# Two mixer layers on one core: output gate summed on VectorE and spread by a transfer, with a new work list

## Chip, core and metric

One core of a Trainium2 chip runs the whole program. The metric is device time in microseconds, the median of several runs. Engine names are those of the profile: PE (matmul), PEld (its weight loads), DVE (vector), ACT (scalar), POOL (GpSimd), SP (the engine whose queue issues every transfer here).

## What is computed

Two layers (DEPTH 2) over 512 latent tokens and 256 context tokens, width 1024. In each layer the normalised and modulated input goes through one wide projection, three attention branches run side by side, each branch is multiplied by a SiLU gate path and projected to 1024, the three are merged by sigmoid gates, and an output projection follows. Shift, scale and **gate** of a layer come from one vector product:

```python
shift, scale, gate = jnp.split(jax.nn.silu(c) @ w_ada[l] + b_ada[l], 3, axis=-1)
h = rms_norm(x, norm_g[l]) * (1.0 + scale[:, None]) + shift[:, None]
...
y = (jax.nn.sigmoid(g_na) * ((o_na * jax.nn.silu(z_na)) @ w_br_l[0])
     + jax.nn.sigmoid(g_mla) * ((o_mla * jax.nn.silu(z_mla)) @ w_br_l[1])
     + jax.nn.sigmoid(g_diff) * ((o_diff * jax.nn.silu(z_diff)) @ w_br_l[2]))
x_new = x + gate[:, None] * (y @ w_out_l)
```

The context stream has its own gate (from c_ctx) and is updated in layer 0 alone. All numbers are float32.

## The kernel before, in words

A float32 product of accuracy is made of three PE products of split operands: every operand is a pair (hi, lo), and `mm3` issues lines 115, 116 and 117. Weights are loaded in units of 128x384 (`ws`, line 138), copied to hi by ACT (line 122) and subtracted to lo by DVE or POOL (line 127).

A layer has twelve steps, one for each pair of heads of the kinds D, M, N in turn. A step of `mixer` records, in this order: the attention of the step before (`attn_group`: scores L712 or L754, softmax, transposes L702, products with V L833 or L867), the projection of this step (`proj_nd` or `proj_m`, PSUM banks `pj`; transposes L473, L662), its SiLU path (`zgate`), some strips of the merge gates (`gm`, 24 in a layer, as many a step as the table `NGM` says), and some halves of the next modulation vectors (`ada_half`, at the steps that `ADA` lists: eight products of `sT` with two weight tiles `aw` of 512 KB, line 237, then the four partial sums of a 256-wide chunk go to `rowsd` in DRAM). `zgate`, `gm` and `ada_half` share one PSUM bank, `fl`: the next user waits until DVE (`zs`, L414), ACT (`th`, L1011) or DVE (`arow`, L239) has read the last one's.

After the steps: for `NE[l]` of the eight output strips the branches 2 and 1 are projected (`branch`) while the last attention runs; then branch 0 of these strips and all three branches of the rest; each finished strip is split into `y` (L122, L127); then `out_proj`, which multiplies by `gate` (L1059), adds to x and stores.

The order on each engine is not the order of recording. Every call sets a priority with `at` (the step's base, plus `PRI` for the kind of work, plus `SHIFT` for single steps), and a scheduler that models the engines picks, while the program is built, what each engine does next by priority and readiness. Each engine then runs its list strictly in order; so does SP's queue of transfers. `NGM`, `SHIFT`, `ADA`, `PRI` and `NE` are thus the **work list**.

The gate before: `ada_gate` (L278) runs after the branches. For each half of 512 columns it loads the partial sums, nine rows with the bias (`arow`, one buffer), and PE multiplies them by a 0/1 matrix `selb`, which sums the rows and spreads the sum over 128 partitions at once (L292); ACT scales it into `gate` (L293). Layer 0 has two streams, layer 1 one: six products of 512 columns, which the profile counts as twelve, since each float32 one is recorded as two.

Of the kernel before, what the change touches and what calls it, by code (L numbers as in the profile page):

```python
# [7 lines left out]
F32 = mybir.dt.float32  # L8
F32R = mybir.dt.float32r
AF = mybir.ActivationFunctionType  # L10
ALU = mybir.AluOpType
AX = mybir.AxisListType

BACC = dict(dynamic_dma_scratch_size=1024)
P = 128
D = 1024
# [10 lines left out]
NEG = -1e30  # L27
BAND = (0, 64, 192, 256)
QTYPE = (0, 1, 1, 2)
NGM = ((1, 3, 0, 2, 4, 0, 0, 4, 3, 2, 3, 2), (0, 4, 1, 0, 2, 1, 1, 4, 2, 3, 4, 2))  # L30

SHIFT = {(12, 'gm'): -1000, (8, 'zg'): -300, (18, 'gm'): -1000, (13, 'attn'): 300, (9, 'zg'): -300, (5, 'pm'): -600, (6, 'attn'): -1000, (23, 'zg'): -600, (8, 'attn'): 150, (10, 'gm'): -1000, (8, 'gm'): -1000}
ADA = ((4, 5, 5, 5, 7, 7, 8, 8, 8, 8, 10, 11), (4, 4, 6, 6))

C_ID = 0
C_ONE = 128
# [12 lines left out]
def f(ap):  # L49
    return ap.bitcast(F32)  # L50


class Mixer:
# [26 lines left out]
    def at(self, key, i=0):  # L80
        o = self.PRI[key] + SHIFT.get((self.where, key), 0)
        self.tc.cur_priority = self.base + o + i * self.PRI["step"] // 20

# [14 lines left out]
    ONE, PF, VG, MR = False, '', '', False  # L98
    COPY, NORM = 'D', 'g'
    PH = ""  # L100
    PRI = dict(step=2200, attn=500, prep=1000, pm=1500, pn=1200, zg=1500, gm=2500, ada=2500, us=300, br=2700)
    ORDER = ('DMNDMNDMNDMN', 'DMNDMNDMNDMN')
    GRP = (0, 1, 2)
    PREP = 0
# [173 lines left out]
    def ada_gate(self, l, pool):  # L278
        nc = self.nc
        strs = (0, 1) if l == 0 else (0,)  # L280
        gate = [pool.tile([P, D], F32, tag=f"gate{s}", bufs=1, name=f"gate{l}_{s}") for s in strs]
        selb = pool.tile([9, 2, P], F32, tag="selb", bufs=1, name=f"selb{l}")
        nc.sync.dma_start(selb, self.io["selb"])
        for hf in range(2):
            rows = pool.tile([9, 512], F32, tag="arow", bufs=1, name=self.n("arow"))
            src = self.rowsd[l][4 + hf].rearrange("k (g r) n -> g r k n", g=4)
            for s in range(2):
                nc.sync.dma_start(rows[4 * s:4 * s + 4, :].rearrange("g (k n) -> g k n", k=4), src[:, s])
            nc.sync.dma_start(rows[8:9, :], self.io["b_gate"][l:l + 1, hf * 512:(hf + 1) * 512])
            for s in strs:  # L290
                ps = self.bk()
                nc.tensor.matmul(ps, selb[:, s, :], rows[0:9, :], start=True, stop=True)  # L292
                nc.scalar.mul(gate[s][:, hf * 512:(hf + 1) * 512], ps, 0.25)  # L293
        return gate

    def bias_gather(self, l):
# [577 lines left out]
    POOLS = dict(pt2=1, th=1, qn=2, sq=2, t2=2, c2=2, c3=2, kr=2, krt=2, mss=2, ssr=2, ss=2)  # L874
    BUFS = dict(pf=1, mr=1, arow=1, qk=6, kl=1, V=5, P=3, pt4=4, pt2=2, zs=2, ut=3, sq=1, ss=4, qn=3, st=3, t2=1, r0=2, th=1, c2=2, c3=1, mss=4, krt=2, Vs=1, bias=1, kr=1, ssr=1)
    BI = {"N": 0, "M": 1, "D": 2}
    NE = (3, 8)

    def open(self, name, side="left"):
        c = self.tc.tile_pool(name=name, bufs=1, side=side, reuse_waits="tile")  # L880
# [2 lines left out]
    def mixer(self, l):  # L883
        tc = self.tc
        ud = self.dram.tile([3, 4, P, NTOK], F32, name=f"ud{l}")
        self.th = self.dram.tile([24, P, NTOK], F32, name=f"thd{l}")
        cs, ps = zip(*(self.open(f"p1{x}_{l}") for x in "abc"))
        pool = _Pool(ps, self.BUFS, self.POOLS)
        gms = list(range(24))
        ada = [(0, 4), (0, 5), (1, 2), (1, 0), (1, 3), (1, 1)] if l == 0 else [(1, 4), (1, 5)]  # L890
        ada = [(*c, hf) for c in ada for hf in range(2)]
        self.base = tc.cur_priority
        br = {"D": self.dtab, "N": dict(pool=pool), "M": None}
        self.kl = pool.tile([P, 2, NTOK], F32R, tag="kl", name=f"kl{l}")
        for m in range(2):
            self.nc.gpsimd.memset(f(self.kl[64 - 64 * m:128 - 64 * m, m]), 0.0)
        prev = None
        seen = dict(D=0, M=0, N=0)
        for step, kind in enumerate(self.ORDER[l]):
            pr = seen[kind]  # L900
            self.where = 12 * l + step
            if l == 0 and step in (0, 6):
                self.bias_gather(step // 6)
            if kind == "N" and pr == 0:
                self.flush()
            seen[kind] += 1
            if prev:
                self.at("attn")
                self.attn(l, *prev, pool, ud)
            if step == self.PREP:  # L910
                self.at("prep")
                self.nbg = self.NB[1]
                br["M"] = self.mla_prep(l, pool, pool)
                self.nbg = self.NB[2]
            if kind == "M":
                self.at("pm")
                a = self.proj_m(l, pr, pool, br[kind])
            else:
                self.at("pn")
                a = self.proj_nd(l, kind, pr, pool, br[kind])  # L920
            self.at("zg")
            prev = (kind, pr, a, self.zgate(l, 4 * self.BI[kind] + pr, None, pool))
            for g in range(NGM[l][step]):
                self.at("gm", g)
                self.gm(l, gms.pop(0), pool)
            for i in range(ADA[l].count(step)):
                self.at("ada", 10 * i)
                self.ada_half(*ada.pop(0), pool)
            self.base += self.PRI["step"]
        assert not gms and not ada  # L930
        for c in cs[:0:-1]:
            c.__exit__(None, None, None)
        self.hctx.__exit__(None, None, None)
        cu, pu = self.open(f"p2u_{l}", "right")
        cx, px = self.open(f"p2x_{l}", "right")
        cf, self.pf2 = self.open(f"p2f_{l}", "right")
        self.at("attn")
        self.attn(l, *prev, pool, ud)
        us = {}
        self.at("us")  # L940
        for b in (2, 1):
            us[b] = self.uload(l, ud, b, pu, px)
        yf = []
        for n in range(self.NE[l]):
            self.at("br", n)
            yf.append(self.branch(l, n, (2, 1), us, px, None, (self.pj, self.fl)))
        cs[0].__exit__(None, None, None)
        tc.cur_priority = self.base + 6000
        cy, py = self.open(f"p2_{l}")
        o = self.cols(l)[0][0]  # L950
        y = [py.tile([P, KT, NTOK], F32R, name=f"y{l}_{j}") for j in range(2)]
        cn, pn = self.open(f"p2n_{l}")
        us[0] = self.uload(l, ud, 0, pn, px)
        for n in range(KT):
            if n < self.NE[l]:
                v = self.branch(l, n, (0,), us, px, yf[n], (self.pj, self.fl, self.bk))
            else:
                v = self.branch(l, n, (2, 1, 0), us, px, None, (self.pj, self.fl, self.bk))
            for c0, w in self.cols(l):
                c = slice(c0, c0 + w)  # L960
                self.split(y[0][:, n, c], y[1][:, n, c], v[:, c0 - o:c0 - o + w], "a", "v")
        gate = self.ada_gate(l, py)
        for c in (cn, cf, cx, cu):
            c.__exit__(None, None, None)
        self.out_proj(l, y, gate)
        cy.__exit__(None, None, None)
# [12 lines left out]
    def branch(self, l, n, bs, us, pool, yf, banks):  # L979
# [3 lines left out]
        if first:  # L983
            yf = self.pf2.tile([P, NTOK - o], F32, tag="yf", bufs=self.NE[l], name=self.n("yf"))
        for b in bs:
# [204 lines left out]
```

## Time and profile before

| what | value |
|---|---|
| median of 3 runs | 1928.85 us (1923.16, 1928.85, 1929.49) |
| the profiled execution | 1923.38 us, its span 1921.6 us |
| granted PE clock, mean | 0.993 |
| PE busy | 1857.9 us (97%) |
| PEld busy | 1725.0 us (90%) |
| DVE, ACT, POOL busy | 1192.0, 938.8, 762.1 us |
| transfers | 245.38 MB, all issued by SP |

The span runs from the first to the last instruction; the execution's own time is 1.8 us longer. PE's rows are pipelined: a product's row lasts longer than the distance to the next one, so the cost of a product is read from the distance of two starts.

### The profile page before, as it was taken

Reading aid. Unit: us, or ns where it says so; the run is one execution under the profiler, and the core shown is the slowest. Engines: PE = TensorE matmul, PEld = TensorE weight load, DVE = VectorE, ACT = ScalarE, POOL = GpSimd, SP = SyncE. Lnnn points to the kernel's source line nnn. Section 1 sums busy time; section 2 is a strip of 40 time slices with the busy share of each in tenths; the row PEclk is TensorE's granted clock in tenths of the full one; section 3 lists DMA queues with packets and bytes.
Section 4 is the critical chain, followed back from the end, with each engine's and each line's share of the span. In section 5 each row is a group of like instructions: output and inputs, shape, how many; then the busy total and the mean of one; then the engine's idle time right before and its main releaser. Section 6 shows DMA issues by size and latency. Waiting matters only on the chain.

```text
span 1921.6 us, 33888 instructions
## 1 busy us (share of the span) xinstructions
PE 1857.9 (97%) x11707; PEld 1725.0 (90%) x11707; DVE 1192.0 (62%) x2698; ACT 938.8 (49%) x2422; POOL 762.1 (40%) x1057
## 2 busy tenths in 40 slices
PE   7999999999999999999999999999899999999998
PEld 3999999999899998999999988898799798889878
DVE  4556567646865655557663455668668665766763
ACT  4445455445644544546432344556456455555531
POOL 3343333233433333243355454444334343443363
PEclk8999999999999999999999999999999999999999
DMA  9454223343545334324655234423522523442663
GB/s 314 159 178 142 64 67 100 102 132 86 159 136 169 85 120 134 103 89 120 228 161 171 99 122 132 122 75 91 167 64 71 161 78 92 123 131 60 192 194 117
DMA packets 184824, 245.38 MB, mean 128 GB/s; under 512 B 22454, under 2 KB 148040, under 8 KB 184652
## 3 DMA queue, kind: packets, MB, share of 16 engines
q1 hardware_dynamic: 184652, 243.21, 41.1%
q8 instruction: 93, 1.52, 0.3%
q14 instruction: 79, 0.65, 0.1%
HBM read 190.45 MB, written 46.53 MB: 123 GB/s over the span
## 4 chain that ended last, share of the span: by engine, by line
PE 87%; DVE 4%; DMA 3%; ACT 2%; POOL 2%; issue 1%; SPq 0%; ACTq 0%; DVEq 0%; POOLq 0%
PE pj L115 11%; PE pj L117 11%; PE pj L116 11%; PE fl L115 10%; PE fl L116 10%; PE fl L117 9%; PE sc L712 6%; PE bk L867 4%; PE bk L702 4%; PE bk L833 2%; PE sc L754 1%; PE pj L662 1%; DMA aw<-in_w_ada 1%; PE pj L473 1%; PE fl L237 1%
## 5 line engine op out<-in xcount | busy, mean ns | idle before, releaser
L122 ACT CAST w<-ws 128x384 fp32r<-128x384 f32 (+3 forms) x520 | 237.4, 473 | 256.2 <-PE fl L116 153.0
L127 POOL TENSOR_TENSOR w<-ws,w 128x384 fp32r<-128x384 f32 (+3 forms) x260 | 242.5, 938 | 298.3 <-ACT w L122 275.3
L115 PE MATMUL fl<-h,w 128*128 128x384 f32 (+1 forms) x864 | 314.4, 364 | 6.4 <-DVE zs L414 4.7
L115 PE MATMUL pj<-w,h 128*128 128x384 f32 (+2 forms) x944 | 313.6, 335 | 2.0 <-DVE kl L127 1.1
L117 PE MATMUL fl<-h,w 128*128 128x384 f32 (+1 forms) x864 | 310.7, 360 | 2.2 <-DVE w L127 1.3
L116 PE MATMUL pj<-w,h 128*128 128x384 f32 (+2 forms) x944 | 309.8, 329 | 1.0 <-POOL w L127 1.0
L116 PE MATMUL fl<-h,w 128*128 128x384 f32 (+1 forms) x864 | 310.0, 359 | 0.0
L117 PE MATMUL pj<-w,h 128*128 128x384 f32 (+2 forms) x944 | 309.2, 331 | 0.7 <-POOL h L127 0.6
L127 DVE TENSOR_TENSOR w<-ws,w 128x384 fp32r<-128x384 f32 (+2 forms) x260 | 170.6, 659 | 72.4 <-ACT w L122 67.2
L167 POOL TENSOR_TENSOR ss<-ss,nhalf 128x4 f32<-128x4 f32 (+1 forms) x144 | 143.1, 994 | 177.8 <-DVE ss L166 161.7
L717 ACT ACTIVATE P<-sc,st 128x768 f32<-128x768 f32 (+1 forms) x192 | 159.5, 832 | 100.8 <-DVE st L798 43.0
L764 POOL TENSOR_SCALAR P<-P,st 128x512 f32<-128x512 f32 (+1 forms) x128 | 107.9, 845 | 241.1 <-DVE st L760 211.4
L115 PEld LDWEIGHTS pj<-w,h 128*128 128x128 f32 x944 | 178.5, 190 | 8.9 <-issue 3.0
L117 PEld LDWEIGHTS pj<-w,h 128*128 128x128 f32 x944 | 177.7, 189 | 5.7 <-DVE h L368 3.3
L115 PEld LDWEIGHTS fl<-h,w 128*128 128x128 f32 x864 | 163.1, 189 | 20.2 <-DVE zs L414 6.5
L116 PEld LDWEIGHTS pj<-w,h 128*128 128x128 f32 x944 | 179.1, 190 | 1.7 <-POOL w L127 1.3
L706 DVE TENSOR_TENSOR pt<-bk,pt 128x512 fp32r<-128x512 f32 (+1 forms) x256 | 147.5, 585 | 52.1 <-ACT pt L705 49.6
L117 PEld LDWEIGHTS fl<-h,w 128*128 128x128 f32 x864 | 162.9, 189 | 14.0 <-POOL w L127 1.6
L116 PEld LDWEIGHTS fl<-h,w 128*128 128x128 f32 x864 | 163.1, 189 | 9.5
L705 ACT CAST pt<-bk 128x512 fp32r<-128x512 f32 (+1 forms) x256 | 127.2, 507 | 77.0 <-PE bk L702 73.9
L712 PE MATMUL sc<-qk,qk 96*128 96x512 f32 (+3 forms) x592 | 144.3, 337 | 1.4 <-ACT P L717 1.0
L702 PE MATMUL bk<-cst,P 128*128 128x128 f32 x832 | 128.9, 273 | 5.0 <-DVE ss L166 2.0
(239 smaller groups left out, 3915.5 us busy)
## 6 DMA issues: line engine op xcount, KB each, us to landing
ws<-in_w_qkv SPq DMA_DIRECT2D x128, 192.0 KB
ws<-in_w_gm SPq DMA_DIRECT2D x96, 192.0 KB
aw<-in_w_ada SPq DMA_DIRECT2D x32, 512.0 KB
ct<-cqd SPq DMA_DIRECT2D x40, 384.0 KB
ct<-ckd SPq DMA_DIRECT2D x48, 256.0 KB
ws<-in_w_z SPq DMA_DIRECT2D x48, 192.0 KB
thd<-th SPq DMA_DIRECT2D x48, 192.0 KB
ws<-in_w_br SPq DMA_DIRECT2D x48, 192.0 KB
```

Of the source, the lines that this page charges most:

```text
L115: mm(out, a[0], b[0], start=first, stop=False)
L116: mm(out, a[0], b[1], start=False, stop=False)
L117: mm(out, a[1], b[0], start=False, stop=last)
L122: nc.scalar.copy(hi, src)
L127: (nc.gpsimd if le == "g" else nc.vector).tensor_tensor(lo, src, f(hi), ALU.subtract)
L167: nc.gpsimd.tensor_tensor(out, out, self.nhalf[:, :cols], ALU.pow)
L702: nc.tensor.transpose(pt[:, i * P:(i + 1) * P], src[:, (b0 + i) * P:(b0 + i + 1) * P], self.ident)
L705: nc.scalar.copy(h, v)
L706: nc.vector.tensor_tensor(lo, v, f(h), ALU.subtract)
L712: mm(s[:, d0:d0 + w], x, y, start=i == 0, stop=i == len(ops) - 1)
L717: nc.scalar.activation(p, src, AF.Exp, bias=st[:, m:m + 1], accum_out=st[:, o:o + 1])
L764: nc.gpsimd.tensor_scalar(p, p, st[:, 4 + m:5 + m], 0.0, ALU.mult, ALU.add)
```

## The change

1. `ada_gate` no longer uses PE or ACT. The four partial sums and the bias go to 8 partitions a stream (`grow`), one DVE reduction adds the five, one DVE instruction scales by 0.25, the 8x128 result is stored to DRAM (`gated`), and a transfer per stream reads it back with every partition reading the same 4 KB (`gate`, 128x1024, 512 KB written). `selb` is no longer loaded.
2. `ada_gate` is called ahead of the branch-0 loop instead of behind it.
3. The work list: `NGM`, `SHIFT`, `ADA`, `PRI["br"]` (2700 to 2600) and `NE` ((3, 8) to (3, 6)) have other values. The number of products in all is the same, apart from the gate's.

```diff
@@ -27,10 +27,10 @@
 NEG = -1e30
 BAND = (0, 64, 192, 256)
 QTYPE = (0, 1, 1, 2)
-NGM = ((1, 3, 0, 2, 4, 0, 0, 4, 3, 2, 3, 2), (0, 4, 1, 0, 2, 1, 1, 4, 2, 3, 4, 2))
-
-SHIFT = {(12, 'gm'): -1000, (8, 'zg'): -300, (18, 'gm'): -1000, (13, 'attn'): 300, (9, 'zg'): -300, (5, 'pm'): -600, (6, 'attn'): -1000, (23, 'zg'): -600, (8, 'attn'): 150, (10, 'gm'): -1000, (8, 'gm'): -1000}
-ADA = ((4, 5, 5, 5, 7, 7, 8, 8, 8, 8, 10, 11), (4, 4, 6, 6))
+NGM = ((1, 3, 0, 2, 3, 0, 0, 4, 3, 2, 3, 3), (1, 4, 0, 0, 2, 1, 1, 4, 1, 3, 4, 3))
+
+SHIFT = {(12, 'gm'): -1000, (8, 'zg'): -150, (18, 'gm'): -1000, (13, 'attn'): 300, (9, 'zg'): -300, (5, 'pm'): -600, (6, 'attn'): -1000, (23, 'zg'): -600, (8, 'attn'): 600, (10, 'gm'): -1000, (8, 'gm'): -1000, (20, 'zg'): -300, (15, 'ada'): 300, (9, 'gm'): 600, (11, 'attn'): 600, (3, 'attn'): 1000, (4, 'attn'): -300}
+ADA = ((5, 5, 5, 6, 7, 7, 8, 8, 8, 9, 10, 11), (4, 4, 6, 6))
 
 C_ID = 0
 C_ONE = 128
@@ -98,7 +98,7 @@
     ONE, PF, VG, MR = False, '', '', False
     COPY, NORM = 'D', 'g'
     PH = ""
-    PRI = dict(step=2200, attn=500, prep=1000, pm=1500, pn=1200, zg=1500, gm=2500, ada=2500, us=300, br=2700)
+    PRI = dict(step=2200, attn=500, prep=1000, pm=1500, pn=1200, zg=1500, gm=2500, ada=2500, us=300, br=2600)
     ORDER = ('DMNDMNDMNDMN', 'DMNDMNDMNDMN')
     GRP = (0, 1, 2)
     PREP = 0
@@ -278,19 +278,20 @@
     def ada_gate(self, l, pool):
         nc = self.nc
         strs = (0, 1) if l == 0 else (0,)
+        n = 8 * len(strs)
         gate = [pool.tile([P, D], F32, tag=f"gate{s}", bufs=1, name=f"gate{l}_{s}") for s in strs]
-        selb = pool.tile([9, 2, P], F32, tag="selb", bufs=1, name=f"selb{l}")
-        nc.sync.dma_start(selb, self.io["selb"])
-        for hf in range(2):
-            rows = pool.tile([9, 512], F32, tag="arow", bufs=1, name=self.n("arow"))
-            src = self.rowsd[l][4 + hf].rearrange("k (g r) n -> g r k n", g=4)
-            for s in range(2):
-                nc.sync.dma_start(rows[4 * s:4 * s + 4, :].rearrange("g (k n) -> g k n", k=4), src[:, s])
-            nc.sync.dma_start(rows[8:9, :], self.io["b_gate"][l:l + 1, hf * 512:(hf + 1) * 512])
-            for s in strs:
-                ps = self.bk()
-                nc.tensor.matmul(ps, selb[:, s, :], rows[0:9, :], start=True, stop=True)
-                nc.scalar.mul(gate[s][:, hf * 512:(hf + 1) * 512], ps, 0.25)
+        gd = self.dram.tile([n, P], F32, name=f"gated{l}")
+        raw = pool.tile([n, 5, P], F32, tag="grow", bufs=1, name=self.n("grow"))
+        src = self.rowsd[l][4:6].rearrange("c k (g r) n -> (c k) g r n", g=4)
+        for s in strs:
+            nc.sync.dma_start(raw[8 * s:8 * s + 8, 0:4], src[:, :, s])
+            nc.sync.dma_start(raw[8 * s:8 * s + 8, 4], self.io["b_gate"][l].rearrange("(k n) -> k n", n=P))
+        tot = pool.tile([n, P], F32, tag="gtot", bufs=1, name=self.n("gtot"))
+        nc.vector.tensor_reduce(tot, raw.rearrange("p g n -> p n g"), AX.X, ALU.add)
+        nc.vector.tensor_scalar(tot, tot, 0.25, None, ALU.mult)
+        nc.sync.dma_start(gd, tot)
+        for s in strs:
+            nc.sync.dma_start(gate[s], gd[8 * s:8 * s + 8].rearrange("k n -> (k n)").unsqueeze(0).to_broadcast([P, D]))
         return gate
 
     def bias_gather(self, l):
@@ -874,7 +875,7 @@
     POOLS = dict(pt2=1, th=1, qn=2, sq=2, t2=2, c2=2, c3=2, kr=2, krt=2, mss=2, ssr=2, ss=2)
     BUFS = dict(pf=1, mr=1, arow=1, qk=6, kl=1, V=5, P=3, pt4=4, pt2=2, zs=2, ut=3, sq=1, ss=4, qn=3, st=3, t2=1, r0=2, th=1, c2=2, c3=1, mss=4, krt=2, Vs=1, bias=1, kr=1, ssr=1)
     BI = {"N": 0, "M": 1, "D": 2}
-    NE = (3, 8)
+    NE = (3, 6)
 
     def open(self, name, side="left"):
         c = self.tc.tile_pool(name=name, bufs=1, side=side, reuse_waits="tile")
@@ -951,6 +952,7 @@
         y = [py.tile([P, KT, NTOK], F32R, name=f"y{l}_{j}") for j in range(2)]
         cn, pn = self.open(f"p2n_{l}")
         us[0] = self.uload(l, ud, 0, pn, px)
+        gate = self.ada_gate(l, py)
         for n in range(KT):
             if n < self.NE[l]:
                 v = self.branch(l, n, (0,), us, px, yf[n], (self.pj, self.fl, self.bk))
@@ -959,7 +961,6 @@
             for c0, w in self.cols(l):
                 c = slice(c0, c0 + w)
                 self.split(y[0][:, n, c], y[1][:, n, c], v[:, c0 - o:c0 - o + w], "a", "v")
-        gate = self.ada_gate(l, py)
         for c in (cn, cf, cx, cu):
             c.__exit__(None, None, None)
         self.out_proj(l, y, gate)
```

What the new list makes of the engines' order, at the three places that the prediction speaks of. From PE's start up to 267.5 us of the profile, from 1061.1 to 1181.4 and from 1310.6 to 1549.7 PE's list is the same as before; elsewhere it differs.

**PE, layer 0, step 4**, where the SiLU path's bank `fl_890` (read by DVE L414) gives way to the first merge-gate strip in `fl_900`. Before:

```order
L117 MATMUL fl_890_4679<-h0_0_108,w_887_4648 128x384
L712 MATMUL sc_801_4210<-qk_688_3547,qk_687_3546 128x512
L712 MATMUL sc_801_4210<-kl0_484,qk_687_3546 128x512
L712 MATMUL sc_801_4210<-qk_688_3547,qk_687_3546 128x256
L712 MATMUL sc_801_4210<-kl0_484,qk_687_3546 128x256
L702 MATMUL bk_788_4158<-cst_69,P_787_4153 128x128 x4
L702 MATMUL bk_789_4165<-cst_69,P_787_4153 128x128 x2
L115 MATMUL fl_900_4724<-h0_0_108,w_892_4708 128x384
```

Now, from behind the last product into `fl_890` (which is followed by four transposes and five products like the first five here) to the first one into `fl_900`:

```order
L117 MATMUL pj_858_4483<-w_820_4309,ct_859_4484 128x192
L115 MATMUL pj_858_4483<-w_823_4317,ct_859_4484 128x192
L116 MATMUL pj_858_4483<-w_824_4318,ct_859_4484 128x192
L117 MATMUL pj_858_4483<-w_823_4317,ct_859_4484 128x192
L115 MATMUL pj_858_4483<-w_826_4323,ct_860_4495 128x256
L116 MATMUL pj_858_4483<-w_827_4324,ct_860_4495 128x256
L841 MATMUL bk_794_4195<-cst_69,dsq_793_4192 128x1 x2
L117 MATMUL pj_858_4483<-w_826_4323,ct_860_4495 128x256
L115 MATMUL pj_858_4483<-w_829_4329,ct_860_4495 128x256
L116 MATMUL pj_858_4483<-w_830_4330,ct_860_4495 128x256
L117 MATMUL pj_858_4483<-w_829_4329,ct_860_4495 128x256
L115 MATMUL fl_900_4724<-h0_0_108,w_892_4708 128x384
```

Four score products and six transposes stood between the two banks; now four transposes and fifteen projection products do.

**PE, layer 1, the end of the branches** (`pj_4654` and `pj_4652` are the last strip's branch 0; `pj_4683` and `pj_4677` the first tile of the output projection). Before:

```order
L116 MATMUL pj_4654_23022<-uT_4589_22786,w_4652_23018 128x512
L117 MATMUL pj_4654_23022<-uT_4588_22785,w_4653_23019 128x512
L292 MATMUL bk_4656_23046<-arow_4655_23042,selb1_23040 128x512
L115 MATMUL pj_4683_23119<-w_4660_23073,y1_0_22762 128x256
L116 MATMUL pj_4683_23119<-w_4661_23074,y1_0_22762 128x256
L117 MATMUL pj_4683_23119<-w_4660_23073,y1_1_22763 128x256
```

Now:

```order
L116 MATMUL pj_4652_23022<-uT_4551_22660,w_4650_23018 128x512
L117 MATMUL pj_4652_23022<-uT_4550_22659,w_4651_23019 128x512
L115 MATMUL pj_4677_23102<-w_4654_23056,y1_0_22636 128x256
L116 MATMUL pj_4677_23102<-w_4655_23057,y1_0_22636 128x256
L117 MATMUL pj_4677_23102<-w_4654_23056,y1_1_22637 128x256
L115 MATMUL pj_4677_23102<-w_4657_23062,y1_0_22636 128x256
```

The gate product L292 is gone. The first output product that reads the last strip of `y` came as the 41st; now it comes as the 54th.

**SP, layer 0, during the branches** (`ws` are branch weights, `tht` merge gates). Before, the gate's transfers stood elsewhere; the second half's, among the output weights:

```order
L138 DMA ws_2623_13570<-in_w_ckv 128x288
L138 DMA ws_2626_13576<-in_w_ckv 128x288
L138 DMA ws_2629_13582<-in_w_ckv 128x288
L138 DMA ws_2632_13588<-in_w_ckv 128x288
L138 DMA ws_2635_13594<-in_w_ckv 128x288
L138 DMA ws_2638_13600<-in_w_ckv 128x288
```

Now:

```order
L988 DMA tht_2374_12246<-thd0_474 128x768
L138 DMA ws_2415_12433<-in_w_br 128x128
L138 DMA ws_2422_12476<-in_w_br 128x384
L138 DMA ws_2425_12482<-in_w_br 128x128
L138 DMA ws_2431_12518<-in_w_br 128x384
L138 DMA ws_2434_12524<-in_w_br 128x128
L988 DMA tht_2383_12290<-thd0_474 128x768
L988 DMA tht_2393_12339<-thd0_474 128x768
L138 DMA ws_2440_12562<-in_w_br 128x384
```

The store `gated0` and the two transfers `gate0` that read it stand in the queue of the branch loads; the first of the two waits for the store's landing and for the last attention product of PE, and all loads behind wait with it. In layer 1 one such transfer stands in the same place, with `ws_4616` as the next load.

## Rows read from the trace of the kernel before

**Rows 1.** The page: busy time (part 1) and the chain's shares (part 4).

```profile
PE 1857.9 (97%) x11707; PEld 1725.0 (90%) x11707; DVE 1192.0 (62%) x2698; ACT 938.8 (49%) x2422; POOL 762.1 (40%) x1057
PE 87%; DVE 4%; DMA 3%; ACT 2%; POOL 2%; issue 1%; SPq 0%; ACTq 0%; DVEq 0%; POOLq 0%
```

**Rows 2.** Busy time by stretch: us; PE, PEld, DVE, ACT, POOL busy (instructions); clock; DMA; GB/s.

```profile
0.00:267.50 267.50, 247.66 (x1521) 225.80 (x1521) 159.68 (x389) 127.65 (x335) 98.65 (x149) 0.97 0.52 164
267.50:1061.10 793.60, 780.02 (x5122) 748.95 (x5121) 481.53 (x1077) 380.55 (x985) 292.76 (x408) 1.00 0.42 127
1061.10:1181.40 120.30, 114.94 (x703) 109.35 (x701) 67.28 (x160) 53.47 (x148) 60.72 (x79) 0.98 0.35 114
1181.40:1310.60 129.20, 127.68 (x789) 115.84 (x789) 84.89 (x205) 66.60 (x173) 51.97 (x74) 0.99 0.34 101
1310.60:1549.70 239.10, 225.76 (x1452) 201.44 (x1451) 170.10 (x401) 132.99 (x348) 104.20 (x156) 0.99 0.40 121
1549.70:1900.00 350.30, 344.90 (x2036) 307.03 (x2035) 222.69 (x462) 177.22 (x436) 150.04 (x188) 1.00 0.40 122
1900.00:1921.60 21.60, 16.93 (x98) 16.61 (x96) 5.86 (x10) 0.32 (x1) 3.74 (x4) 0.99 0.24 98
```

**Rows 3.** PE's waits, 267.5 to 1061.1 us: total us, times, longest.

```profile
PE pj L473 <- DVE qn L467: 3.1, 2, 2.8
PE fl L115 <- DVE zs L414: 2.8, 3, 1.6
PE fl L115 <- ACT th L1011: 1.2, 4, 0.4
PE fl L237 <- DVE V L523: 1.1, 1, 1.1
```

**Rows 4.** PE's waits, 1549.7 to 1921.6 us.

```profile
PE pj L117 <- DVE y L127: 1.3, 1, 1.3
```

**Rows 5.** Timeline of PE at step 4's bank change: start, us, what, [idle before, releaser].

```profile
355.98 0.82 PE L702 MATMUL bk<-cst,P 128*128 128x128 f32 x6
358.35 0.44 PE L115 MATMUL fl<-h,w 128*128 128x384 f32 x1 [1.55 <-DVE zs L414]
```

**Rows 6.** Timeline of PE at 737 us, step 9's last transposes.

```profile
737.85 0.41 PE L473 MATMUL pj<-cst,qn 128*128 128x128 f32 x2 [2.77 <-DVE qn L467]
```

**Rows 7.** Timeline of PE round the gate products of both layers.

```profile
1022.43 0.33 PE L116 MATMUL pj<-uT,w 128*128 128x384 f32 x1
1022.60 0.34 PE L117 MATMUL pj<-uT,w 128*128 128x384 f32 x1
1022.87 1.12 PE L292 MATMUL bk<-arow,selb 9*128 9x512 f32 x2
1023.92 0.39 PE L115 MATMUL pj<-w,y 128*128 128x256 f32 x1
...
1876.02 0.28 PE L117 MATMUL fl<-w,y 128*128 128x256 f32 x1
1876.14 0.28 PE L116 MATMUL pj<-w,y 128*128 128x256 f32 x1
1876.85 1.09 PE L292 MATMUL bk<-arow,selb 9*128 9x512 f32 x2 [0.43 <-DMA arow<-in_b_gate]
1877.87 0.38 PE L117 MATMUL pj<-w,y 128*128 128x256 f32 x1
```

**Rows 8.** The chain of waits, 1866 to 1880 us: start, us, what.

```profile
1871.91 4.80 DMA arow<-in_b_gate
```

**Rows 9.** The chain of waits, whole span: a load of 512 KB.

```profile
1490.73 7.41 DMA aw<-in_w_ada
```

**Rows 10.** Tile adat: min/median/max ns, first and last start.

```profile
L253 DVE TENSOR_REDUCE adat<-adar x1: 1029/1029/1029, 1033.6 to 1033.6; 32x128 f32<-32x512 f32 x1
```

**Rows 11.** Timeline of PEld in the branch stage, where PE waits for nothing.

```profile
1860.20 0.19 PEld L117 LDWEIGHTS bk<-uT,w 128*128 128x128 f32 x1
1860.42 0.19 PEld L115 LDWEIGHTS bk<-uT,w 128*128 128x128 f32 x1
```

## The prediction

> **What bounds the kernel now.** I read the page first, then PE by stretches, then PE's waits, then single places. PE is busy 97% of the span and holds 87% of the chain that ended last; DVE, the next, is busy 62% [rows 1]. So time is won in two ways alone: fewer PE cycles, or less idle PE. The stretches say how much idle PE the change can reach. PE's list is the same as before in three of the seven stretches of [rows 2], and there its idle time (length less PE busy) stays: 19.8 us at the start, 5.4 us at 1061, 13.3 us at 1311 to 1550. Where the list differs, PE idles 13.6, 1.5 and 5.4 us, 20.5 us in all. The last 4.7 us lie behind the last product, where only results leave; nothing is changed there. All that the new work list can win by filling PE is therefore 20.5 us, about 1% of the span, and it starts from a list that leaves 1.6% of these 1273 us idle.
>
> Durations come from one execution of 1923.4 us (span 1921.6). The median of the three runs shown is 1928.85, so the profiled run lies 5.5 us low among its like; the sum is made against 1923.4, and the range allows for that scatter. A measurement of this kernel tells a change from none from about 0.3%, 5.8 us.
>
> **The change, part by part.**
>
> *The gate leaves PE.* A pair of L292 rows is one product of 512 columns. In layer 0 the products around the first pair start at 1022.60 and 1023.92: 1.32 us, less the ordinary step of 0.17, is 1.15 us for the pair [rows 7]. In layer 1 the pair at 1876.85 takes 1.73 us from start to start, less a step of 0.12: 1.6 us, because PE also waited 0.43 us for the bias row [rows 7], which landed 4.80 us after its issue [rows 8]. Five pairs at 1.15 and one at 1.6 make 7.4 us; a little less where two pairs stand together. I take 7. Bounds: at the least 4.6 (the four pairs of layer 0), if both of layer 1's only lengthen the wait for `y` that follows them; at the most 7.4.
>
> *ACT and DVE.* ACT loses six small instructions. DVE gains two reductions and two scalings. The nearest row is the reduction of 32x512 to 32x128 in 1.03 us [rows 10]; one of 16x640 reads a quarter more, so 1.3 us at the most, with a shorter scaling behind it. That is some 2 us a layer on an engine that is idle for 38%. Cost nothing: PE has several strips of weights ahead in that stage. If that cover were gone, 4 us.
>
> *The spread by transfers.* Three transfers write 512 KB each. The nearest row is a load of 512 KB, which ended a wait 7.41 us after issue [rows 9]. They run beside the branch loads. The new waits are SP's: the store of the sum must land before the read of it may be issued, and in both layers the read also waits for PE's last attention product. Every later load stands behind these. The first of them in layer 0 is a part of the weights that PE reads 213 products of 384 columns after the attention's end, by the order 37 us at 0.17 us each; in layer 1 it is 110 products of 512, 25 us at 0.22 to 0.23 us, the distance of the loads in [rows 11]. The blockage itself is one landing of about 4.80 us [rows 8] and one or two transfers of 7.41 [rows 9]: at most 19.6 and 12.2 us, below 37 and 25. Cost nothing; the other end of this price is a rival. The gather in layer 1 also waits for PE's end of attention and has the last two loads for branch 0 behind it, but before the change the load of `selb` waited for the same there, ahead of all four.
>
> *The work list, layer 0.* Its PE waits by name [rows 3]: 3.1 us for the projection's `qn`, 2.8 and 1.2 us for the one `fl` bank, 1.1 us before an `ada` half, and a tail of small ones. The bank waits can be judged by the order. The largest is 1.55 us at 358 us, where 4 score products and 6 transposes were all that hid ACT and DVE reading the bank [rows 5]; now 15 products of about 0.12 us (the step in [rows 7]) and 4 transposes stand there, about 2 us, more than the 1.55 us that were lacking, so it goes. Counted over the changed stretch, the handovers of the bank with under 1.2 us of products between are 11 before and 10 now, and the four waits on `th` come to 1.2 us in all [rows 3]. I credit 2 us of the bank waits. The largest `qn` wait, 2.77 us [rows 6], stays: behind the last projection product of step 9 there still stands one `ada` half and nothing more. So does the `ada` wait before it. Of the small ones I take half, 2 us.
>
> *The work list, layer 1.* The 1.3 us for the last strips of `y` [rows 4]: without the gate PE arrives 1.15 us earlier, but 13 more products of 0.12 us now stand ahead of the last strip. I credit half, 0.7 us. `NE` from 8 to 6 moves the products of branches 2 and 1 of two strips behind the last attention; step 11's merge-gate strips take their place, so the cover there stays about the same. I credit 1 us for the other waits of these stretches.
>
> That is some 6 us of waits gone. A new list has new waits at places that I can't foresee by counting; I set 1 us against it. Bounds of the list: a gain of 20.5 us (all idle time gone) and a loss; at the density of the unchanged stretch from 1311 to 1550, 13.3 us in 239 [rows 2], these 1273 us would idle 71 us, 50 more than now. I stay near no change, since the count of short handovers hardly moved.
>
> **Sum:** 1923.4 − 7 (gate) − 5 (list) = 1911.4, **1911 us**.
>
> One rule speaks for more. By the rows, PE is idle for 64 us, PEld for 197 [rows 1 and 2]. The Trainium skill ("Perfetto Trace Analysis", Identifying the Most-Contended Engine) holds that matmul busy time is a poor measure of the headroom and the busy share of weight loads a better one, since products are pipelined; by that, the changed stretches would hold 101 us of headroom and not 20. The trace here bears it out only in part: in the branch stage the loads last 0.19 us and start 0.22 us apart with no wait at all [rows 11], so a seventh of PEld's time is idle there by the width of the product alone.
>
> **The rivals.**
>
> *A: only the gate counts.* The list swaps waits for waits. For: the handover counts are 11 and 10, and the large `qn` and `ada` waits keep their places. Against: the bank wait at 358 us is plainly covered now. Time 1923.4 − 7 = 1916; with the gate at its lower bound, 1919. This lies across the bound of 0.3%. That the gate stays on PE is no case: no L292 product is left in the new order.
>
> *B: SP's queue becomes the bound (slower).* If the branch loads behind the gate's transfers come late, PE pays the blockage: 19.6 us in layer 0 and 12.2 in layer 1, less 7 for the gate: 1923.4 + 24.8 = 1948; with layer 1's alone, 1929. It decides once PE needs the first blocked load earlier than 19.6 (12.2) us after the attention. The Trainium skill ("DMA: Bandwidth & Descriptors", Anatomy of one DMA) has the rule for it: transfer engines do not wait on semaphores, the issuing engine waits before it dispatches, so one dependent transfer holds up all later ones of that engine. The 4.80 us of [rows 8] is such a landing. Against: 37 and 25 us of cover by the order.
>
> *C: the list fills nearly all of the idle time.* 1923.4 − 7 − 20.5 = 1896. For: the rule on weight loads above. Against: the waits that keep their places, 2.77 us and others.
>
> **How the numbers follow.** My forecast (gate, and some of the waits: 1903 to 1916) has 0.55; A 0.25, of which 0.10 lies beyond the bound; C 0.12; B, or a list that makes more waits than it removes, 0.08, of which 0.02 ends within the bound. Faster by over 0.3%: 0.55 + 0.10 + 0.12 = 0.77. Within: 0.15 + 0.02 = 0.17. Slower: 0.06. The range leaves out the better half of C and most of B: 1899 to 1924, the upper end being A's 1919 and the scatter of the runs.
>
> **What would show it.** The L292 and L293 rows are gone and PE's busy time falls by about 6 us. PE's waits on `zs` at 358 us are gone, the wait of 2.77 us for `qn` at the end of step 9 is there. In the branch stage no `ws` load becomes a releaser of ACT's copies; if one does, right behind the `gate` transfers, B holds. Idle PE in the changed stretches falls from 20.5 to about 15 us. A span that falls by under 4 us, or by over 24, proves the sum wrong; so does a stretch with an unchanged list that moves by more than 2 us.

## Result and profile after

| | executions | median us | ratio to before, 95% |
|---|---|---|---|
| before | 4 | 1926.01 | |
| changed | 4 | 1904.14 (1901.39 to 1905.57) | 0.9886 (0.9859 to 0.9913) |
| changed, measured again | 6 | 1904.34 (1900.41 to 1905.86) | 0.9888 (0.9868 to 0.9907) |

The kernel became 1.1% faster, 21 to 22 us. The forecast was 1911, the range 1899 to 1924. Profile against profile the gain is 1923.38 − 1904.18 = 19.2 us where the sum said 12: the sign and the two sources of the gain hold, the size does not.

The page of the changed kernel, busy time, answers to [rows 1]: PE lost 13.0 us of busy time, DVE gained 8.3. Of the 13.0 us, 4.4 lie in the start and 1.7 in the stretch up to 1549 us, where PE's list is as before. Of the 8.3, the gate's four instructions on DVE are 3.8.

```profile
PE 1844.9 (97%) x11695; PEld 1722.8 (91%) x11695; DVE 1200.3 (63%) x2702; ACT 936.1 (49%) x2416; POOL 766.8 (40%) x1057
```

The stretches of the changed kernel, cut at the same products as [rows 2] (columns as there):

```profile
0.00:264.20 264.20, 243.22 (x1521) 225.13 (x1521) 159.87 (x389) 127.47 (x335) 98.15 (x149) 0.99 0.53 166
264.20:1047.70 783.50, 775.06 (x5115) 748.30 (x5113) 481.71 (x1078) 378.05 (x981) 295.06 (x408) 1.00 0.43 130
1047.70:1168.60 120.90, 114.91 (x703) 109.42 (x701) 66.86 (x160) 53.35 (x148) 60.62 (x79) 0.99 0.35 114
1168.60:1298.40 129.80, 128.92 (x788) 116.30 (x789) 86.07 (x206) 67.59 (x173) 51.76 (x74) 0.99 0.34 101
1298.40:1534.60 236.20, 224.07 (x1450) 200.61 (x1449) 170.13 (x401) 132.89 (x348) 104.46 (x156) 0.99 0.40 122
1534.60:1879.30 344.70, 341.91 (x2032) 306.61 (x2031) 229.95 (x464) 176.53 (x434) 153.10 (x188) 1.00 0.41 125
```

Read against [rows 2], line by line: the start is 3.3 us shorter although PE's list there is as before. Layer 0 (second line) is 10.1 us shorter: PE busy 780.02 to 775.06 and idle 13.6 to 8.4. The next two stretches are 0.6 longer each. The stretch with layer 1's unchanged list is 2.9 us shorter. The last attention, branches and output projection are 5.6 shorter: PE busy −3.0, idle 5.4 to 2.8. So in the three stretches with a new list PE idles 12.1 us instead of 20.5.

PE's waits in layer 0 of the changed kernel (total us, times, longest), to be read beside [rows 3]:

```profile
PE fl L237 <- DMA aw<-in_w_ada: 1.7, 2, 1.3
PE fl L115 <- DVE arow L239: 1.4, 1, 1.4
PE fl L115 <- DVE zs L415: 0.9, 1, 0.9
PE pj L474 <- DVE qn L468: 0.8, 1, 0.8
PE fl L115 <- ACT th L1012: 0.2, 1, 0.2
```

`zs` fell from 2.8 to 0.9, `th` from 1.2 to 0.2, `qn` from 3.1 to 0.8; a wait for `arow` of 1.4 and one for a load of `aw` are new.

The new gate, on DVE (the tile `gtot`: min/median/max ns) and on SP's queue (start us, us, what), changed kernel:

```profile
L290 DVE TENSOR_REDUCE gtot<-grow x2: 1299/1302/1305, 944.9 to 1817.3; 16x128 f32<-16x640 f32 x1, 8x128 f32<-8x640 f32 x1
L291 DVE TENSOR_SCALAR gtot<-gtot x2: 207/614/1021, 947.9 to 1819.2; 16x128 f32<-16x128 f32 x1, 8x128 f32<-8x128 f32 x1
```

```profile
949.32 0.37 SPq L292 DMA_DIRECT2D gated<-gtot  x1
949.79 0.36 SPq L988 DMA_DIRECT2D tht<-thd  x1
950.59 0.34 SPq L138 DMA_DIRECT2D ws<-in_w_br  x1
952.58 0.80 SPq L294 DMA_DIRECT2D gate<-gated  x2
953.47 0.86 SPq L138 DMA_DIRECT2D ws<-in_w_br  x2
...
1819.63 0.32 SPq L292 DMA_DIRECT2D gated<-gtot  x1
1820.06 0.33 SPq L988 DMA_DIRECT2D tht<-thd  x1
1820.48 0.37 SPq L138 DMA_DIRECT2D ws<-in_w_br  x1
1822.04 0.32 SPq L294 DMA_DIRECT2D gate<-gated  x1
```

The store and the read of it are issued 3.3 and 2.4 us apart, and other loads are issued between them. Between the two SP stands still for 1.65 us at most in layer 0 (950.93 to 952.58) and 1.2 in layer 1; the bound of the prediction was 19.6 and 12.2.

### The profile page after: what moved, and what is told of

Same layout as the page of the kernel before. It is cut to its first block, busy times and chain, and to the rows that moved or that the text cites. A ratio compares the mean times of both kernels' runs of the same rounds, so it can differ in the third digit from the quotient of the medians.

```text
span 1901.0 us, 33889 instructions
## 1 busy us (share of the span) xinstructions
PE 1844.9 (97%) x11695; PEld 1722.8 (91%) x11695; DVE 1200.3 (63%) x2702; ACT 936.1 (49%) x2416; POOL 766.8 (40%) x1057
## 5 line engine op out<-in xcount | busy, mean ns | idle before, releaser
L127 DVE TENSOR_TENSOR w<-ws,w 128x384 fp32r<-128x384 f32 (+2 forms) x260 | 178.1, 689 | 62.4 <-ACT w L122 59.6
```

What stands on the lines that cost most here:

```text
L127: (nc.gpsimd if le == "g" else nc.vector).tensor_tensor(lo, src, f(hi), ALU.subtract)
```

## The experiments

The theory after the first reading: the gate is worth the PE time of its products, the new list somewhat more than the prediction gave it, and the two add. The rivals: gate and list only work together; or part of the 22 us is nothing that the change did.

What decides is often not the median (the interval of a ratio is 0.12 to 0.2% on either side, 2 to 4 us, and that of a difference of two ratios is wider) but the length of a stretch, taken between the starts of the same two products in each trace. This table is worked out so; the places are the products that start at 266.6, 1062.4, 1312.2, 1549.3 and 1916.6 us before the change.

| kernel (one profile each) | to 266 | layer 0, to 1062 | to 1312 | to 1549 | to the last product |
|---|---|---|---|---|---|
| before | 266.6 | 795.7 | 249.8 | 237.1 | 367.3 |
| changed | 263.4 | 785.6 | 251.0 | 234.4 | 361.5 |
| changed, again | 264.0 | 784.2 | 250.2 | 234.7 | 361.8 |
| gate alone | 268.2 | 795.2 | 248.8 | 233.5 | 366.5 |
| list alone | 262.9 | 789.3 | 250.9 | 233.9 | 364.1 |
| gate, layer 0's list | 264.7 | 784.6 | 250.3 | 239.5 | 366.1 |
| gate, layer 1's list | 266.1 | 794.9 | 249.8 | 239.8 | 363.3 |
| changed, NE (3, 8) | 264.2 | 785.2 | 249.9 | 239.1 | 365.5 |
| changed, gate called late | 264.4 | 785.5 | 250.5 | 239.5 | 361.7 |

**The gate alone**: the kernel before with `ada_gate` and its call as in the change, the list old.

```diff
         us[0] = self.uload(l, ud, 0, pn, px)
+        gate = self.ada_gate(l, py)
...
-        gate = self.ada_gate(l, py)
```

> Gate new and called ahead of the loop, work list old. Theory G7: the gate is worth the PE time of its products alone, 7 us (4.6 to 7.4), ratio 0.996, about 1919 us against 1926; the stretches in which PE's list is as before move by less than 1 us each, the one up to 267 us of the profile too unless its 3.3 us are scatter between executions. Rival (the gate brings most of the 22 us, since banks, ACT and SP's queue come free too): 1909 or less, ratio 0.991. Rival (the gate was hidden behind the last wait for y): 1924 to 1926.

Measured: 1919.19 us, ratio 0.9971 (0.9958 to 0.9985), about 5.6 us of 1924, by the interval 2.9 to 8.1. The rival that gives the gate most of the gain falls, and so does the one that hides it. Where the 5.6 us lie is not shown by this profile. Layer 0, which lost four of the six products, is only 0.5 us shorter: PE is busy 2.9 us less and idle 2.3 us more. Part of that is the clock: from 740.0 to 743.4 us the granted clock is 0.52, which the profile of before has nowhere in this column. The last column falls by 0.8 us, and 3.6 us lie in the stretch up to 1549 us, which holds no gate product. In layer 1 PE's waits of this kernel from 1546 to 1917 us show what came in the place of the products:

```profile
PE fl L115 <- DVE tht L999: 1.8, 1, 1.8
PE pj L117 <- DVE y L127: 1.2, 1, 1.2
```

The wait for `y` is as long as in [rows 4]; it did not grow. The wait for a branch's merge gate did, from 0.8 us before to 1.8. One expectation missed: stretches with an untouched list moved by up to 3.6 us.

**The list alone**: the changed kernel with `ada_gate` and its call as before.

```diff
-        gate = self.ada_gate(l, py)
         for n in range(KT):
...
+        gate = self.ada_gate(l, py)
         for c in (cn, cf, cx, cu):
```

> New work list, gate as before with PE products. Theory G7: the list alone brings 12 to 15 us, ratio 0.993, 1911 to 1914 us; the two parts add up to the whole. Rival (list as in the prediction): 5 us, 1921 us. Rival (list and gate only work together): over 1922.

Measured: 1913.02 us, ratio 0.9934 (0.9919 to 0.9949), 12.7 us. The list is the larger part, over twice the 5 us of the prediction. Without the new gate PE's idle time falls as in the changed kernel: in layer 0 to 7.9 us (13.6 before, 8.4 changed), in the last column to 2.8 (5.4 before, 2.8 changed). On top of the list the gate brings 0.9934 − 0.9888, about 8.8 us; with both intervals that is not told apart from the 5.6 us that it brought alone. In the table it takes layer 0 from 789.3 to 785.6 and the last column from 364.1 to 361.5, 2.6 us, where with layer 1's old list it took 0.8.

**The list of one layer**: the changed kernel with the old list in layer 1 (the diff shows two of the lines; the SHIFT entries for steps 12 to 23 are old too), and the other way round, with layer 0's NGM, ADA and SHIFT entries old and layer 1's and NE new. `PRI["br"]`, which both layers share, stays new in both.

```diff
-NGM = ((1, 3, 0, 2, 3, 0, 0, 4, 3, 2, 3, 3), (1, 4, 0, 0, 2, 1, 1, 4, 1, 3, 4, 3))
+NGM = ((1, 3, 0, 2, 3, 0, 0, 4, 3, 2, 3, 3), (0, 4, 1, 0, 2, 1, 1, 4, 2, 3, 4, 2))
...
-    NE = (3, 6)
+    NE = (3, 8)
```

> New gate, new list in layer 0 alone (steps 0 to 11 and the bound of the branches), old list and NE in layer 1. From the two traces the list brings about 5.5 us in layer 0 (267 to 1061 us of the profile less the gate's 4.6): with the gate's 7 us, 1913 to 1914 us, ratio 0.9935. Rival (layer 0's list is neutral and all of it is layer 1's): 1919, ratio 0.996.

> New gate, old list in layer 0, new list and NE in layer 1. From the two traces layer 1's list brings about 5.5 us (2.9 in the stretch 1310 to 1550 where PE's own list is unchanged, 3 behind it): with the gate 1913 to 1914 us. Rival (the 2.9 us of the unchanged stretch are scatter, or follow from layer 0): 1916 to 1919.

Measured: 1910.96 us, ratio 0.9929 (0.9911 to 0.9947), with layer 0's list; 1914.77 us, 0.9955 (0.9940 to 0.9970), with layer 1's. Less the gate alone (0.9971) that is 8.1 us for layer 0's list and 3.1 for layer 1's, each uncertain by about 4 us, so that the medians alone do not tell layer 1's part from nothing. The table decides: in the column of layer 0 the old list takes 795 us with the new gate and the new list 784.2 to 785.6, two profiles against five. PE's idle time there is 15.9 and 14.0 us in the two, 8.2 to 8.8 in the five. In the last column it is 5.8 us with layer 1's old list and 3.0 with the new one. That column also shows how few profiles the gate's part in layer 1 stands on: with the old list of layer 1 it takes 0.8 and 1.2 us (366.5 and 366.1 against 367.3), with the new one 2.6 in the changed kernel, but 0.8 here (363.3 against 364.1), where the granted clock fell to 0.72 from 1790 to 1796 us. The 2.9 us of the stretch up to 1549 us are layer 1's list by none of these runs: with it 239.8, without it 233.5 and 239.5.

**The changed kernel again**, with more executions.

> The changed kernel once more, with more executions. Its four executions so far had a mean granted clock of 0.994 to 0.995, those of before 0.990 to 0.996. Theory: the true gain is what the parts add up to, 5.5 (gate) + 8 (layer 0's list) + 3 to 4 (layer 1's), about 17 to 18 us, and the 22 us measured first hold 3 to 4 us of luck with the clock: median 1906 to 1908, ratio 0.990 to 0.991, and mean clocks down to 0.991 among the executions. Rival: the new list itself keeps the clock up: median 1904, ratio 0.9886 again, clocks 0.994 and up.

Measured: 1904.34 us, 0.9888 (0.9868 to 0.9907). The expectation of 1906 to 1908 missed; the rival had the time right (1904), but not the clocks, which lie between 0.992 and 0.996. The parts give 5.6 + 8.1 + 3.1 = 16.8 us, the whole 21.5. The gap of 4.7 us is within the noise of the four ratios, some 6 us. The larger share of the gate in layer 1 with the new list (2.6 us against 0.8) does not belong in it: the 3.1 us of layer 1's list were measured with the new gate and hold it already. The granted clock can be part of the gap: its mean over the 10 executions of the changed kernel is 0.9939, over 48 of before in all comparisons 0.9925, and among before's own executions the median falls from 1926.0 at a clock of 0.991 (12 executions) to 1920.6 at 0.995 (8), 1.35 us for each 0.001. By that the difference of the means is worth some 2 us. Whether the new list keeps the clock up or these executions were lucky isn't settled: the mean of the kernels with one part is 0.9920 to 0.9932.

**Halves of the modulation vectors spread**: one `ada` half a step in layer 1, against the waits for `aw` there.

```diff
-ADA = ((5, 5, 5, 6, 7, 7, 8, 8, 8, 9, 10, 11), (4, 4, 6, 6))
+ADA = ((5, 5, 5, 6, 7, 7, 8, 8, 8, 9, 10, 11), (4, 5, 6, 7))
```

> The changed kernel with the halves of the modulation vectors in layer 1 at steps 4, 5, 6 and 7 instead of 4, 4, 6, 6. Theory: PE waits for the weight tiles of the second half of a pair because both tile buffers are still in use by the first (2.7 us at step 16, 2.7 us at step 18, and the clock falls behind them), so with one half a step these waits go: 4 to 6 us less than the changed kernel. Rival: the loads are late for another reason (SP's queue or the transfers' share), and the waits stay: within 1 us. Second rival: the scheduler's new order of the other work makes new waits of the same size.

Measured: 1906.20 us, ratio 0.9895 (0.9873 to 0.9916), not told apart from the changed kernel. The wait for `aw` between 1298 and 1535 us, 4.7 us in the changed kernel, is gone from the list of this one, as the theory said. New waits took its place, the largest at the end of the attention (timeline of PE):

```profile
1771.83 0.98 PE L115 MATMUL pj<-uT,w 128*128 128x512 f32 x3 [2.35 <-ACT uT L122]
```

ACT waited there for the load of `uraw`, which SP issued behind three loads of `ws`:

```profile
1760.28 6.98 SPq L138 DMA_DIRECT2D ws<-in_w_br  x3
1767.91 1.75 SPq L975 DMA_DIRECT2D uraw<-ud  x4
```

But the load is no later than in the changed kernel, where it is issued at 1768.59 us behind `ws` too. What differs is PE's order: there twelve products with V come ahead of this place (1768.40 to 1771.0 us), here twelve come behind it. The second rival holds: a wait that goes in one place comes back in another.

**NE as before**, and **the gate called late**, both in the changed kernel.

```diff
-    NE = (3, 6)
+    NE = (3, 8)
```

> The changed kernel with NE (3, 8) as before: in layer 1 the branches 2 and 1 of all eight strips ahead of the end of the last attention. Theory: fewer products lie between the last attention and out_proj, so the wait for y of some 1.4 us comes back and the length from 1534 us to the last product is 1.5 to 3 us longer (363 to 364.5 instead of 361.5). Rival: the other entries of the list removed that wait and NE is neutral: 361 to 362.

```diff
-        gate = self.ada_gate(l, py)
         for n in range(KT):
...
+        gate = self.ada_gate(l, py)
         for c in (cn, cf, cx, cu):
```

> The changed kernel with ada_gate called behind the branch-0 loop as before. Theory: only the place of a few transfers in SP's queue changes, and the first user of gate comes tens of us later: every stretch within 1 us of the changed kernel. Rival: the later place makes out_proj wait for gate, or holds other loads back: 2 us or more in the stretch behind the attention of either layer.

One execution each, 1910.92 us with NE (3, 8) and 1910.69 with the late call. With NE (3, 8) the last column is 365.5 us instead of 361.5 and 361.8, beyond the 363 to 364.5 that were expected, and among PE's waits from 1543 us on are the one for `y`, which the changed kernel does not have, and a further one for `uT`:

```profile
PE pj L117 <- DVE y L127: 1.2, 1, 1.2
PE bk L115 <- ACT uT L122: 1.1, 1, 1.1
```

So by this one profile NE alone is worth some 4 us of layer 1, 2.6 of them idle PE. That it is NE that lets the gate's time be kept there is not shown: no run has the old gate with the old NE and the rest of the list new. With the late call every stretch but one is within 1 us of the changed kernel; the move of the call is worth nothing. The one exception, 239.5 us up to 1549, accounts for most of the 1910.69. It has the same list in both and differs in the clock, 0.96 against 0.99 in the stretches above. The two other long ones that have the list of one layer, 239.5 and 239.8 us, have 0.96 too; the gate alone, with 233.5, has 0.99.

```profile
1301.50:1541.00 239.50, 227.37 (x1438) 203.96 (x1439) 169.02 (x400) 132.17 (x344) 104.16 (x156) 0.96 0.40 121
```

**Half of layer 0's list**: the old SHIFT entries with the new NGM and ADA, and the other way round.

```diff
-(8, 'zg'): -150, (8, 'attn'): 600, (9, 'gm'): 600, (11, 'attn'): 600, (3, 'attn'): 1000, (4, 'attn'): -300
+(8, 'zg'): -300, (8, 'attn'): 150
```

> The changed kernel with layer 0's entries of SHIFT and nothing else as before (NGM, ADA, PRI and NE new, layer 1 new). The new list of layer 0 is worth 8 to 9 us. Theory: it works as a whole, the scheduler's order with half of it holds new waits: 5 to 9 us slower than the changed kernel, waits over 0.6 us in layer 0 back at 11 us or more. Rival (NGM and ADA bring it): within 2 us of the changed kernel.

```diff
-NGM = ((1, 3, 0, 2, 3, 0, 0, 4, 3, 2, 3, 3), (1, 4, 0, 0, 2, 1, 1, 4, 1, 3, 4, 3))
+NGM = ((1, 3, 0, 2, 4, 0, 0, 4, 3, 2, 3, 2), (1, 4, 0, 0, 2, 1, 1, 4, 1, 3, 4, 3))
...
-ADA = ((5, 5, 5, 6, 7, 7, 8, 8, 8, 9, 10, 11), (4, 4, 6, 6))
+ADA = ((4, 5, 5, 5, 7, 7, 8, 8, 8, 8, 10, 11), (4, 4, 6, 6))
```

> The changed kernel with layer 0's NGM and ADA as before and its SHIFT entries new. Theory (as a whole): 5 to 9 us slower than the changed kernel. Rival (SHIFT brings it): within 2 us. If both this and the run with the old SHIFT are 4 us or so slower, the two halves add up.

Measured: 1920.81 us, ratio 0.9990 (0.9978 to 1.0002), with the old SHIFT; 1916.76 us, 0.9973 (0.9962 to 0.9985), with the new SHIFT alone. The whole old list of layer 0 gave 0.9955. Half of the new list is thus worse than none of it, by 7 and by 3 us; the 7 are clear of the noise, the 3 lie at its edge. The traces say the same of both: measured as in the table, layer 0 takes 798.9 and 798.0 us, with PE idle for 19.8 and 20.5, where the whole old list with the new gate took 795 and idled 14.0 and 15.9. Against the changed kernel they are some 20 and 16 us slower by the ratios, 13 of it in layer 0; the 5 to 9 us that were expected were too few. PE's waits in layer 0 (264 to 1063 us), old SHIFT first, show new ones at new places, as the theory had it:

```profile
PE fl L115 <- DVE zs L415: 3.5, 4, 1.6
PE fl L115 <- DVE arow L239: 2.0, 2, 1.4
PE pj L663 <- DVE qn L657: 1.9, 1, 1.9
```

```profile
PE fl L237 <- DMA aw<-in_w_ada: 6.4, 5, 1.9
PE pj L474 <- DVE qn L468: 3.7, 2, 2.8
PE pj L115 <- ACT sq L449: 2.1, 1, 2.1
```

**Eight more round trips** between the store of the sum and its spreading: rival B, forced.

```diff
         nc.sync.dma_start(gd, tot)
+        for i in range(8):
+            t2 = pool.tile([n, P], F32, tag="gtot", bufs=1, name=self.n("gtot"))
+            nc.sync.dma_start(t2, gd)
+            gd = self.dram.tile([n, P], F32, name=f"gated{l}_{i}")
+            nc.sync.dma_start(gd, t2)
```

> The changed kernel with eight more round trips of the 8x128 sum through DRAM, one behind the other, between the store of the sum and its spreading, in both layers. Each holds SP's queue for two landings, 3 to 5 us by the changed kernel's trace (store to dependent read 3.3 us), about 55 us in all in each layer. Theory (cover of 37 us in layer 0, 25 us in layer 1 by the order): PE pays what lies over it, about 18 us and 30 us, 1904 + 48 = 1952 us, and ACT's copies of branch weights wait for their loads right behind the round trips. Rival (no cover, every blocked us is paid): 110 us, 2014 us. Rival (SP's queue never matters, the loads are far ahead): under 1910 us.

Measured: 1913.7 us, one execution. None of the three numbers, but nearest to the third (under 1910, the queue never matters): the scheduler put other loads between the trips, so SP was held in many short pieces and not in one long one.

```profile
947.76 0.35 SPq L292 DMA_DIRECT2D gated<-gtot  x1
...
950.60 0.32 SPq L295 DMA_DIRECT2D gtot<-gated  x1
952.89 0.32 SPq L297 DMA_DIRECT2D gated<-gtot  x1
953.30 0.85 SPq L138 DMA_DIRECT2D ws<-in_w_br  x2
...
981.71 0.80 SPq L299 DMA_DIRECT2D gate<-gated  x2
```

The chain lasts 34 us in layer 0. From 1312 us on the length is that of other profiles up to 1549 (239.7), and the last column is 366.4, 4.8 us more than the changed kernel's; layer 0 takes 786.8, 1.2 to 2.6 more. The largest new wait of PE is for weights of the output projection, and the copy of such weights on ACT just before had waited 2.30 us for their load. That is the kind of wait that rival B described, one stage later (timeline of PE):

```profile
1861.44 0.39 PE L116 MATMUL pj<-w,y 128*128 128x256 f32 x1 [1.82 <-DVE w L127]
```

So the rule of the Trainium skill that the prediction quoted ("DMA: Bandwidth & Descriptors", Anatomy of one DMA) agrees with the trace: a dependent transfer holds the queue (SP issues nothing from 950.92 to 952.89 us, until the store of what was just read). What that costs is far less than the 34 us: by this one profile eight trips cost some 6 to 7 us in both layers together. The one trip of the change costs nothing that these runs show. That the cover makes the difference is argued, not shown.

## Why the prediction was right, and where not

- *The gate leaves PE, 7 us.* PE's busy time in the two stretches fell by 5.0 + 3.0 = 8.0 us. Right with the new list, by busy time. Alone the gate brought 5.6 (2.9 to 8.1), which does not tell the lower bound of 4.6 from 7. The reason given for the bound did not come true: the wait for `y` did not grow with the gate alone, the one for a merge gate did, by 1.0.
- *DVE, 1.3 us at the most and hidden.* Right: 1.30 us. The scaling took 0.2 and 1.0, and the trace names nobody who waited for its result.
- *The spread by transfers, nothing.* Right. The estimate of the blockage by 4.80 and 7.41 us landings [rows 8, 9] was far too high: the small store had landed after 2.4 to 3.3 us at most, and SP issued the next load right behind the reads, without waiting for them to land.
- *Layer 0's bank waits, 2 us.* The wait at 358 us is gone, and `zs` and `th` together fell by 2.9; the new one on `arow` takes 1.4 back.
- *The 2.77 us for `qn` stay.* Half right. The `ada` half stands there as counted, but the wait is 0.78 us now, and the bank behind it costs 1.42, so 0.6 us of waiting are won (rows below); in that execution the fall of the clock behind it cost 1.6. The wait before the `ada` half stayed (1.1 for `V`, now 1.7 for `aw`).
- *Small waits, 2 us, less 1 for new ones.* With the terms above, idle PE in layer 0 fell by 5.2 us where the sum had 4.
- *Layer 1, 0.7 + 1 us.* The term that was most undersized: 3.2 us by idle PE (1.5 to 0.9 and 5.4 to 2.8), and NE alone some 4 by one profile. The prediction said that with NE 6 "the cover there stays about the same"; the wait for `y` went wholly.
- *Idle PE in the changed stretches 20.5 to about 15:* it is 12.1. Of the 8.4 won the sum had 5.
- *An unchanged list moves by under 2 us.* This step failed, as the prediction's own test: 3.3 us at the start and 2.9 up to 1549. It took one profile of a stretch for its length. With the same order of PE the stretch up to 1549 took 233.5 to 239.8 us in the nine profiles of the table, short and long ones under either list of layer 1, and the clock differed there. The start took 262.9 to 268.2, and that is less clear. With layer 0's old SHIFT entries it took 266.1 to 268.2 in all four profiles, with the new ones 262.9 to 264.7 in all nine (the profiles that are not in the table included). Yet up to 266 us the order on every engine is the same before and in the changed kernel, so no run shows how the entries could act there; it may be chance.

So of the 20.6 us by which the span fell from profile to profile, 8.0 go with the gate, 8.4 with the list's idle time, and the rest, 4.2, lies mostly in stretches whose list is unchanged (3.3 and 2.9 won, 2 lost in other places); 1.4 us went back outside the span (1.8 us before, 3.2 after). Among medians the list is worth about 11 to 13 us, uncertain by some 3. The sum undersized it. It credited single waits that could be named, and in layer 0 those came out close; that a new list moves many small ones at once is the likely reason, which no run isolates. Rival A (the list is neutral) falls with the list alone. Rival C (nearly all idle time gone) falls with 12.1 us left. Rival B (SP's queue becomes the bound) does not come about with the one trip of the change; with eight more, 6 to 7 us of it do.

A third buffer for `aw` was not tried. No run here beats the changed kernel.

## What to carry to other kernels

Where one engine is busy 97% of the time, a new order of work is a matter of all its entries together: here half of a good list lost more than it won. Time taken off an engine need not come out of the total: with the old list the gate's last products brought about 1 us of layer 1 and another wait grew; with the new list they brought up to 2.6. Before a difference of 3 us in one stretch is explained, the same stretch should be read in a second profile, with its granted clock beside it. And when parts are added up, it should be clear which of them were measured together.

## What the hardware showed that was not expected

The granted clock explains much of the scatter between executions of one program. Step 9 of the changed kernel (timeline of PE):

```profile
714.13 1.07 PE L237 MATMUL fl<-aw,sT 128*32 128x256 f32 x16
715.99 0.41 PE L474 MATMUL pj<-cst,qn 128*128 128x128 f32 x2 [0.78 <-DVE qn L468]
717.82 0.53 PE L115 MATMUL fl<-h,w 128*128 128x384 f32 x1 [1.42 <-DVE arow L239]
718.14 0.53 PE L116 MATMUL fl<-h,w 128*128 128x384 f32 x1
...
721.57 0.34 PE L115 MATMUL fl<-h,w 128*128 128x384 f32 x1
721.75 0.34 PE L116 MATMUL fl<-h,w 128*128 128x384 f32 x1
```

Behind two waits of 0.78 and 1.42 us the products start 0.32 us apart, eleven of them, and then 0.18 apart: PE ran at 1.2 GHz and then at 2.4 again, which cost about 1.6 us on top of the waits. The granted clock of the two stretches says the same (busy time by stretch, columns as in [rows 2]):

```profile
717.80:721.30 3.50, 3.48 (x11) 3.49 (x12) 1.97 (x5) 0.38 (x2) 2.10 (x3) 0.53 1.06 362
721.60:725.10 3.50, 2.55 (x16) 2.28 (x14) 0.68 (x2) 0.74 (x2) 0.00 (x0) 1.00 0.10 34
```

The waits alone do not decide it. In the changed kernel measured again the same two waits of 0.78 and 1.42 us come at the same place, and the products behind them start 0.17 us apart from the second on. In the profile of before, the longer wait of 2.77 us [rows 6] had no such end, but with the gate alone, whose order is the same there, a wait of 2.76 us had: its granted clock is 0.52 from 740.0 to 743.4 us. The start of the program differs in the same way between two traces with the same order, as busy time from 20 to 40 us shows, before first and changed second (clock in the third column from the right):

```profile
20.00:30.00 10.00, 7.32 (x40) 3.02 (x40) 3.52 (x7) 1.02 (x2) 2.51 (x8) 0.85 1.04 380
30.00:40.00 10.00, 9.74 (x28) 3.80 (x28) 8.67 (x15) 5.89 (x11) 5.17 (x7) 0.64 0.97 315
```

```profile
20.00:30.00 10.00, 6.48 (x46) 3.42 (x48) 3.81 (x9) 1.11 (x3) 2.88 (x9) 1.00 1.05 392
30.00:40.00 10.00, 9.49 (x45) 4.43 (x45) 9.48 (x16) 5.79 (x11) 4.71 (x5) 1.00 0.96 306
```

There before ran 68 products and the changed kernel 91 in the same 20 us; that is the 3.3 us of the first stretch: the same product starts 0.1 us earlier at 26 us, 4.2 at 38, and 3.4 earlier from 46 us on. The kernel with the late call, whose order is the changed kernel's at the start, fell to 0.83 from 20 to 30 us.
